# Softmax heads: the probabilities go unscaled through the product with v, whose result stands by query, is scaled there and transposed back

## The chip, the core and the metric

The kernel is one program on one core of a Trainium2 chip. Its time is the device time of one execution in microseconds (us), a median over several runs. The engines are named as the profile names them: PE is TensorE (matmuls and transposes), PEld its weight loads, DVE is VectorE, ACT is ScalarE, POOL is GpSimd, SP is SyncE, which here issues DMAs.

## The reference, cut to what matters

The whole computation is two transformer blocks over 512 positions of width 1024, in float32. The change lies in the softmax heads of the second block: the four heads of group A (merged dilated causal attention), four of group C (a window of 128 with a sink logit), four of group D (causal blocks) and the four heads of the cross attention into 256 memory tokens. Each computes, with heads of 64 columns:

```python
s = jnp.einsum("bgrnqe,bgnke->bgrnqk", qb, kb) * SCALE + bias[None, :, :, None]
s = jnp.where(valid, s, NEG)
m = jnp.maximum(jnp.max(s, axis=-1, keepdims=True), sink)
p = jnp.exp(s - m)
den = jnp.sum(p, axis=-1, keepdims=True) + jnp.exp(sink - m)
o = jnp.einsum("bgrnqk,bgnke->bgrnqe", p / den, vb)
```

(this is group C; A and D have no sink, the cross attention neither sink nor bias). `p / den` may be taken before the product with v or after it, since `den` belongs to a query.

## The kernel before

Everything is float32. A product of float32 precision is made of three matmuls: both factors are split in a high and a low part (`split`, ACT copies the high part, DVE subtracts), and high*high, high*low and low*high are added up in PSUM (`mm3` and the three matmuls of line 1251). Activations are held with features on the 128 partitions and positions along the row.

`softmax_units` makes one head as four units of 128 queries, two to a pair. A unit goes through these steps, parted by `yield`: (1) two matmuls give the scores with the queries on the partitions (`sc`, line 1206), DVE adds the bias and takes the maximum (1211, in the cross attention 1214); (2) ACT takes the exponent and its sum `den` (1218, 1215), DVE takes the reciprocal of `den` (1223) and multiplies the 128 to 512 probabilities of each query by it (1224); (3) PE transposes the probabilities in blocks of 128 keys to a PSUM tile `tr` (1228); (4) they are split into `pth` and `ptl` (105, 106); (5) for the second unit of a pair, the product with v: v (64 columns) is the stationary operand, the probabilities of both units, 256 queries wide where both see the key block and 128 where one does, are the moving one (1252). The result stands with the head's 64 features on the partitions, as the output projection needs it, and ACT copies it to `y` (1254).

A causal head (A, D) has windows of 1, 2, 3 and 4 key blocks; a head of C has 1, 2, 2 and 2; one of the cross attention 2 each. The `tr` tiles have three PSUM buffers, the scores two.

`weave` (line 1314) starts one unit per step, moves the others that are under way by one step each, and between them issues pieces of "fill": the projections of later groups (`pair`, lines 1393 to 1398), the norm of earlier ones (`finish`), or output projections. So the order of the text is that of the weave; a scheduler then moves instructions of each engine within what dependencies allow. The groups come in the order B (another kind of head, unchanged), A, D, C, and then, in `cross`, the memory heads. In the profiled execution the scores of the changed heads start at 952 us; roughly, A stands before 1000, D from 1000 to 1031, C from 1031 to 1072 with its last steps up to 1080, the cross heads from 1102 to 1149. The MLP with its large matmuls follows up to the end.

Line 1363 makes a constant, `lower`, which is read once, at line 1367, long before the heads.

Of the kernel before, what the change touches and what calls it, by code (L numbers as in the profile page):

```python
# [11 lines left out]
FT = mybir.dt.float32  # L12
FR = mybir.dt.float32r
AF = mybir.ActivationFunctionType
OP = mybir.AluOpType
# [4 lines left out]
P = 128  # L20
# [43 lines left out]
class Net:  # L64
# [1117 lines left out]
    def softmax_units(self, q, ks, v, vc, y, yr, window, bias=None, sink=None, keys=SEQ, tag=lambda pair: pair,  # L1182
                      again=False):

        nc = self.nc
        V = nc.vector
        vh, vl = v
        nkt = keys // P  # L1190
        st = {}

        def unit(ti):
            pair, i = divmod(ti, 2)
            wins = [window(2 * pair + n) for n in range(2)]
            k0, k1 = wins[i]
            f0 = wins[0][0]
            w = (k1 - k0) * P
            if bias is not None and (ti == 0 or again and i == 0):
                st["e"] = self.bt.tile([P, 512], FT, name="bias")  # L1200
                nc.sync.dma_start(st["e"], bias)
            ps = self.psc.tile([P, 512], FT, name="sc")
            qs, q0 = q(pair)
            qs = qs[:, q0 + i * P:q0 + i * P + P]
            for x in range(2):
                nc.tensor.matmul(ps[:, 0:w], qs, ks[x][:, k0 * P:k1 * P], start=x == 0, stop=x == 1)
            p = self.at.tile([P, keys], FT, name="e")[:, 0:w]
            nm, den = (self.at.tile([P, 1], FT, name=n) for n in ("nm", "den"))
            if bias is not None:
                o = 384 - P * ti + P * k0  # L1210
                V.tensor_tensor_reduce(p, ps[:, 0:w], st["e"][:, o:o + w], -1.0, 3.0e38 if sink is None else sink[1],
                                       OP.add, OP.min, nm)
            else:
                V.tensor_reduce(nm, ps[:, 0:w], AX.X, OP.max, negate=True)
                nc.scalar.activation(p, ps[:, 0:w], AF.Exp, bias=nm, accum_out=den)
            yield
            if bias is not None:
                nc.scalar.activation(p, p, AF.Exp, scale=-1.0, bias=nm, accum_out=den)
            if sink is not None:
                e = self.at.tile([P, 1], FT, name="es")  # L1220
                nc.scalar.activation(e, sink[0], AF.Exp, bias=nm)
                V.tensor_tensor(den, den, e, OP.add)
            V.reciprocal(den, den)
            V.tensor_scalar(p, p, den, None, OP.mult)
            yield
            pt = self.ptr.tile([P, 512], FT, name="tr")
            for j in range(k1 - k0):
                nc.tensor.transpose(pt[:, j * P:(j + 1) * P], p[:, j * P:(j + 1) * P], self.ident)
            yield
            if i == 0:  # L1230
                n = wins[1][1] - f0
                k = tag(pair)
                full = 1280 if k and keys == SEQ else 512
                st["p"] = [self.ap.tile([P, full], FR, name=f"{t}{k}")[:, 0:256 * n].rearrange(
                    "p (j t) -> p j t", j=n) for t in ("pth", "ptl")]
            pth, ptl = st["p"]
            src = pt[:, 0:w].rearrange("p (j t) -> p j t", t=P)
            at = (slice(None), slice(k0 - f0, k1 - f0), slice(i * P, (i + 1) * P))
            self.split(pth[at], ptl[at], src)
            if i == 0:  # L1240
                return
            yield
            yp = self.ptr.tile([P, 512], FT, name="tr")

            (a0, a1), (b0, b1) = wins
            both = [j for j in range(nkt) if a0 <= j < a1 and b0 <= j < b1]
            jobs = [(j, 0, 256) for j in both]
            jobs += [(j, 0, P) for j in range(a0, a1) if j not in both]
            jobs += [(j, P, 256) for j in range(b0, b1) if j not in both]
            for ji, (j, c0, c1) in enumerate(jobs):  # L1250
                for x, (m, d) in enumerate(((vh, pth), (vh, ptl), (vl, pth))):
                    nc.tensor.matmul(yp[0:64, c0:c1], m[:, j, vc:vc + 64], d[:, j - f0, c0:c1], start=ji == x == 0,
                                     stop=ji == len(jobs) - 1 and x == 2)
            nc.scalar.activation(y[yr, pair * 256:pair * 256 + 256], yp[0:64, 0:256], AF.Copy)

        return [unit(i) for i in range(4)]

    def stick_units(self, q, ks, v, vc, y, yr):
# [83 lines left out]
    def hybrid(self):  # L1342
        nc = self.nc
        V = nc.vector
        I = self.I
        with ExitStack() as es:
# [3 lines left out]
            yp = self.pool(e2, "yp", 1)  # L1350
# [8 lines left out]
            c = hp  # L1359
            self.strict = c.tile([P, P], FT, name="strict")  # L1360
            nc.gpsimd.affine_select(self.strict, self.ones, pattern=[[1, P]], compare_op=OP.is_gt, fill=0.0, base=0,
                                    channel_multiplier=-1)
            lower = c.tile([P, P], FT, name="lower")
            nc.gpsimd.affine_select(lower, self.ones, pattern=[[-1, P]], compare_op=OP.is_ge, fill=0.0, base=0,
                                    channel_multiplier=1)
            self.ntri = c.tile([P, P], FR, name="ntri")
# [605 lines left out]
```

## Time and profile before

| | |
|---|---|
| median of three runs | 1522.76 us (1522.1 to 1524.31) |
| profiled execution, device time | 1525.71 us |
| its span in the trace | 1524.0 us |
| PE busy | 1464.5 us, 96% of the span |
| PEld busy | 1319.5 us, 87% |
| DVE busy | 1007.3 us, 66% |
| ACT busy | 741.2 us, 49% |
| granted TensorE clock over the span | 0.994 |

Busy time of an engine is the time covered by at least one of its records. Matmuls overlap: one of 256 columns shows some 0.28 us, while the next starts 0.12 us later. So a busy PE can still have room, and what a matmul costs is read from the distance between the starts of neighbours, not from its own length. A weight load (PEld) stands ahead of each matmul and overlaps the matmul before.

### The profile page before, as it was taken

How to read it: one execution, taken by the hardware profiler on the slowest of the kernel's cores; microseconds unless marked ns; L12 is line 12 of the kernel's file. 1: busy time of each engine (PE TensorE's matmuls, PEld its weight loads, DVE VectorE, ACT ScalarE, POOL GpSimd, SP SyncE). 2: the span in 40 equal slices, each digit the busy share in tenths (PEclk: the TensorE clock that was granted, in tenths of full speed). 3: DMA queues.
4: the chain of work that ended last, by engine and by line, in shares of the span. 5: the costliest groups of instructions: out<-in, count | busy, mean ns of one | idle time of the engine just before them, and what ended most of it. 6: DMA issues, size and time to landing. Idle time of an engine off the chain costs nothing.

```text
span 1524.0 us, 25154 instructions
## 1 busy us (share of the span) xinstructions
PE 1464.5 (96%) x9769; PEld 1319.5 (87%) x9769; DVE 1007.3 (66%) x1963; ACT 741.2 (49%) x1437; POOL 284.0 (19%) x321
## 2 busy tenths in 40 slices
PE   7899899999989999999999999999989999999996
PEld 7899899988989999989999988988888888888886
DVE  6988979878587766665474755888896443344334
ACT  5333356655665444444454465686685431144321
POOL 1157821003352111100131211000221000000001
PEclk9999999999999999999999999999999999999998
DMA  6333342226546766643657244314211322233221
GB/s 207 100 100 98 103 114 89 65 69 225 162 140 221 255 229 245 226 136 110 184 155 237 99 152 140 124 43 146 97 57 56 97 96 93 88 98 97 97 83 56
DMA packets 76223, 197.63 MB, mean 130 GB/s; under 512 B 16188, under 2 KB 25644, under 8 KB 75976
## 3 DMA queue, kind: packets, MB, share of 16 engines
q1 hardware_dynamic: 67384, 166.66, 34.9%
q0 software_dynamic: 7632, 28.31, 4.9%
q8 instruction: 77, 1.26, 0.3%
q10 hardware_dynamic: 1088, 1.05, 0.2%
q14 instruction: 42, 0.34, 0.1%
HBM read 171.75 MB, written 28.15 MB: 131 GB/s over the span
## 4 chain that ended last, share of the span: by engine, by line
PE 65%; DVE 7%; ACT 3%; DMA 2%; issue 1%; DVEq 0%; SPq 0%; ACTq 0%
PE mm L146 6%; PE mm L147 6%; PE mm L149 6%; PE mm L176 5%; PE mm L179 5%; PE mm L178 5%; PE mx L176 4%; PE mx L179 4%; PE mx L178 4%; PE mx L146 3%; PE mx L147 3%; PE mx L149 3%; PE mm L1396 2%; PE mm L1395 2%; PE mm L1393 2%; DVE xl L109 1%
## 5 line engine op out<-in xcount | busy, mean ns | idle before, releaser
L127 DVE TENSOR_TENSOR wlo<-wst,whi 128x1024 fp32r<-128x1024 f32 (+3 forms) x244 | 299.2, 1228 | 193.1 <-ACT whi L126 116.9
L126 ACT ACTIVATE whi<-wst 128x1024 fp32r<-128x1024 f32 (+3 forms) x244 | 249.9, 1026 | 283.6 <-PE mm L147 113.8
L178 PE MATMUL mm<-xh,whi 128*128 128x256 f32 (+4 forms) x800 | 229.2, 312 | 3.0 <-DVE vl L109 1.6
L179 PE MATMUL mm<-xl,whi 128*128 128x256 f32 (+4 forms) x800 | 229.6, 313 | 0.2
L178 PE MATMUL mx<-xh,whi 128*128 128x512 f32 (+3 forms) x576 | 174.2, 325 | 8.2 <-ACT xh L108 8.2
L179 PE MATMUL mx<-xl,whi 128*128 128x512 f32 (+3 forms) x576 | 175.0, 326 | 1.3 <-DVE xl L109 1.2
L178 PEld LDWEIGHTS mm<-xh,whi 128*128 128x128 f32 (+1 forms) x800 | 150.6, 188 | 13.0 <-DVE vl L109 1.8
L179 PEld LDWEIGHTS mm<-xl,whi 128*128 128x128 f32 (+1 forms) x800 | 150.2, 188 | 10.5 <-issue 0.6
L176 PE MATMUL mm<-xh,wlo 128*128 128x256 f32 (+4 forms) x800 | 138.2, 312 | 0.0
L146 PE MATMUL mm<-hh,whi 128*128 128x256 f32 (+1 forms) x480 | 132.6, 307 | 0.0
L147 PE MATMUL mm<-hl,whi 128*128 128x256 f32 (+1 forms) x480 | 132.5, 307 | 0.0
L178 PEld LDWEIGHTS mx<-xh,whi 128*128 128x128 f32 x576 | 109.2, 190 | 17.1 <-ACT xh L108 8.5
L176 PEld LDWEIGHTS mm<-xh,wlo 128*128 128x128 f32 (+1 forms) x800 | 115.3, 187 | 9.9 <-issue 0.4
L179 PEld LDWEIGHTS mx<-xl,whi 128*128 128x128 f32 x576 | 108.8, 189 | 11.9 <-DVE xl L109 2.8
L176 PE MATMUL mx<-xh,wlo 128*128 128x512 f32 (+3 forms) x576 | 104.3, 322 | 0.0
L146 PEld LDWEIGHTS mm<-hh,whi 128*128 128x128 f32 x480 | 90.4, 189 | 5.4
L147 PEld LDWEIGHTS mm<-hl,whi 128*128 128x128 f32 x480 | 90.5, 189 | 5.1
L176 PEld LDWEIGHTS mx<-xh,wlo 128*128 128x128 f32 x576 | 86.0, 187 | 9.1
L252 POOL TENSOR_TENSOR nacc<-nacc,sq 128x256 f32<-128x256 f32 (+2 forms) x58 | 56.2, 970 | 202.2 <-ACT sq L251 193.0
L149 PE MATMUL mm<-hh,wlo 128*128 128x256 f32 (+1 forms) x480 | 79.5, 307 | 1.3 <-DVE wlo L127 1.3
L149 PEld LDWEIGHTS mm<-hh,wlo 128*128 128x128 f32 x480 | 67.5, 188 | 6.7 <-DVE wlo L127 1.7
L252 POOL TENSOR_TENSOR acc<-acc,sq 128x264 f32<-128x264 f32 (+1 forms) x6 | 4.3, 741 | 335.3 <-ACT sq L251 335.3
(570 smaller groups left out, 3305.7 us busy)
## 6 DMA issues: line engine op xcount, KB each, us to landing
wst<-in_w_in_dram SPq DMA_DIRECT2D x39, 512.0 KB, 3.5
wst<-in_w_down_dram SPq DMA_DIRECT2D x32, 512.0 KB, 3.5
wst<-in_w_mup_dram SPq DMA_DIRECT2D x32, 512.0 KB, 3.5
wst<-in_w_mdown_dram SPq DMA_DIRECT2D x32, 512.0 KB, 3.7
wst<-in_w_gate_dram SPq DMA_DIRECT2D x22, 512.0 KB, 4.0
wst<-in_w_up_dram SPq DMA_DIRECT2D x22, 512.0 KB, 3.5
wst<-in_w_out_dram SPq DMA_DIRECT2D x20, 512.0 KB, 3.9
ready<-phi POOLq DMA_DIRECT2D x17, 512.0 KB, 3.1
```

What stands on the lines that cost most here:

```text
L126: nc.scalar.activation(hi[:, 0:n], st[:, 0:n], AF.Copy)
L127: nc.vector.tensor_tensor(lo[:, 0:n], st[:, 0:n], hi[:, 0:n].bitcast(FT), OP.subtract)
L146: nc.tensor.matmul(ps, ah, bh, start=start and i == 0, stop=False)
L147: nc.tensor.matmul(ps, ah, bl, start=False, stop=False)
L149: nc.tensor.matmul(ps, al, bh, start=False, stop=stop and i == n - 1)
L176: nc.tensor.matmul(ps, wl[:, k], xh, start=False, stop=k == KT - 1)
L178: nc.tensor.matmul(ps, wh[:, k], xh, start=k == 0, stop=False)
L179: nc.tensor.matmul(ps, wh[:, k], xl, start=False, stop=False)
L252: (nc.vector if k % len(accs) else nc.gpsimd).tensor_tensor(acc[:, c:c + w], acc[:, c:c + w], sq, OP.add)
L1393: nc.tensor.matmul(ps, wl[:, k], xh, start=False, stop=k == KT - 1)
L1395: nc.tensor.matmul(ps, wh[:, k], xh, start=k == 0, stop=False)
L1396: nc.tensor.matmul(ps, wh[:, k], xl, start=False, stop=False)
```

## The change

The reciprocal and the multiplication of the probabilities go, and with them one `yield`, so the transposes come in the same step as the exponent. The sums of a pair's two units are kept side by side in one tile `den` of two columns. The product is turned: the probabilities of one unit and one key block, 128 queries, are the stationary operand, v's 64 columns the moving one, so the result has the queries on the partitions, 64 columns for each of the two units. The reciprocal of both sums is taken at once, DVE multiplies the result by it on its way out of PSUM to `yt`, and two transposes bring it back to 64 features by 128 queries each, in the upper half of the same `tr` tile, from where ACT copies it as before. `lower` moves to a buffer of the bias tiles.

```diff
-            nm, den = (self.at.tile([P, 1], FT, name=n) for n in ("nm", "den"))
+            nm = self.at.tile([P, 1], FT, name="nm")
+            if i == 0:
+                st["den"] = self.at.tile([P, 2], FT, name="den")
+            dens = st["den"]
+            den = dens[:, i:i + 1]
...
-            V.reciprocal(den, den)
-            V.tensor_scalar(p, p, den, None, OP.mult)
-            yield
             pt = self.ptr.tile([P, 512], FT, name="tr")
...
             yield
+
             yp = self.ptr.tile([P, 512], FT, name="tr")
-
-            (a0, a1), (b0, b1) = wins
-            both = [j for j in range(nkt) if a0 <= j < a1 and b0 <= j < b1]
-            jobs = [(j, 0, 256) for j in both]
-            jobs += [(j, 0, P) for j in range(a0, a1) if j not in both]
-            jobs += [(j, P, 256) for j in range(b0, b1) if j not in both]
-            for ji, (j, c0, c1) in enumerate(jobs):
-                for x, (m, d) in enumerate(((vh, pth), (vh, ptl), (vl, pth))):
-                    nc.tensor.matmul(yp[0:64, c0:c1], m[:, j, vc:vc + 64], d[:, j - f0, c0:c1], start=ji == x == 0,
-                                     stop=ji == len(jobs) - 1 and x == 2)
-            nc.scalar.activation(y[yr, pair * 256:pair * 256 + 256], yp[0:64, 0:256], AF.Copy)
+            for n, (j0, j1) in enumerate(wins):
+                for j in range(j0, j1):
+                    for x, (m, d) in enumerate(((vh, pth), (vl, pth), (vh, ptl))):
+                        nc.tensor.matmul(yp[:, 64 * n:64 * n + 64], d[:, j - f0, n * P:(n + 1) * P],
+                                         m[:, j, vc:vc + 64], start=j == j0 and x == 0, stop=j == j1 - 1 and x == 2)
+            V.reciprocal(dens, dens)
+            yield
+            yt = self.at.tile([P, 2, 64], FT, name="yt", bufs=2)
+            V.tensor_tensor(yt, yp[:, 0:128].rearrange("p (n c) -> p n c", n=2),
+                            dens.unsqueeze(2).to_broadcast([P, 2, 64]), OP.mult)
+            yield
+            for n in range(2):
+                nc.tensor.transpose(yp[0:64, 256 + n * P:256 + (n + 1) * P], yt[:, n], self.ident)
+            nc.scalar.activation(y[yr, pair * 256:pair * 256 + 256], yp[0:64, 256:512], AF.Copy)
...
-            lower = c.tile([P, P], FT, name="lower")
+            lower = bt.tile([P, 512], FT, name="bias")[:, 0:P]
```

In the built program PE has 232 matmuls and transposes more, DVE 64 instructions fewer; the other engines have as many as before. Lines of the changed kernel are four higher after the change, some within it lower; 1248 are its products, 1250 the reciprocal, 1253 the scaling, 1257 the transposes back.

On PE, the product of the first pair of the first A head, before (`e` are the probabilities, `pth` and `ptl` their split transposes, `v2h` and `v2l` the parts of v, `sc` scores):

```order
L1228 MATMUL tr<-ident,e 128x128 x3
L1252 MATMUL tr<-pth_11310,v2h 64x256
L1206 MATMUL sc<-kh,qs 128x512
L1252 MATMUL tr<-ptl_11311,v2h 64x256
L1252 MATMUL tr<-pth_11310,v2l 64x256
L1252 MATMUL tr<-pth_11310,v2h 64x128
L1252 MATMUL tr<-ptl_11311,v2h 64x128
L1252 MATMUL tr<-pth_11310,v2l 64x128
L1228 MATMUL tr<-ident,e 128x128 x4
```

and the start of the same product now:

```order
L1397 MATMUL mm<-xh_8559,wlo 128x512
L1397 MATMUL mm<-xh_8560,wlo 128x512
L1228 MATMUL tr<-ident,e 128x128 x3
L1248 MATMUL tr<-v2h,pth_11287 128x64
L1248 MATMUL tr<-v2l,pth_11287 128x64
L1248 MATMUL tr<-v2h,ptl_11288 128x64
```

Six matmuls of 256 or 128 columns have become nine of 64 (the three at the end of the piece stand three times in a row), in one block.

On PE in the D heads, around the second pair of one head, now (`yt` is the scaled result, `rs` the norm of an earlier group):

```order
L1228 MATMUL tr_11782<-ident_78,e_11723 128x128 x2
L1228 MATMUL tr_11805<-ident_78,e_11788 128x128 x3
L305 MATMUL rs_12590<-ident_78,rsr_12581 128x128 x4
L1257 MATMUL tr_11754<-ident_78,yt_11800 64x128 x2
L1205 MATMUL sc_12105<-kh_11628,qs_11501 128x256
L1205 MATMUL sc_12105<-kl_11629,qs_11501 128x256
L1205 MATMUL sc_12153<-kh_11628,qs_11501 128x384
L1205 MATMUL sc_12153<-kl_11629,qs_11501 128x384
L1248 MATMUL tr_11839<-v2h_10546,pth0_11777 128x64
```

Between a product and its transposes back stand the transposes of later units; between those and the next product, four score matmuls.

On DVE, in the A heads, before:

```order
L1211 ISA e,nm<-sc,bias 128x384
L1211 ISA nm 128x1
L1223 RECIPROCAL den<-den 128x1
L1224 TENSOR_SCALAR e<-e,den 128x256
L1223 RECIPROCAL den<-den 128x1
L1224 TENSOR_SCALAR e<-e,den 128x384
```

and now, at the first scaling of a result:

```order
L1250 RECIPROCAL den<-den 128x2
L1214 ISA e,nm<-sc,bias 128x384
L1214 ISA nm 128x1
L106 TENSOR_TENSOR ptl_11359<-tr,pth_11358 128x3x128
L1253 TENSOR_TENSOR yt<-tr,den 128x128
L1214 ISA e,nm<-sc,bias 128x512
```

Two operations for each unit have become two for each pair, and they have moved from ahead of the transposes to behind the product.

## Rows read from the trace of the kernel before

**Rows 1.** The page: the span, busy time and share of two engines, and the chain of work that ended last, by engine.
```profile
span 1524.0 us, 25154 instructions
PE 1464.5 (96%) x9769; PEld 1319.5 (87%) x9769; DVE 1007.3 (66%) x1963; ACT 741.2 (49%) x1437; POOL 284.0 (19%) x321
...
PE 65%; DVE 7%; ACT 3%; DMA 2%; issue 1%; DVEq 0%; SPq 0%; ACTq 0%
```

**Rows 2.** The view of busy time by stretch: stretch in us, its length, busy time and instructions of PE, PEld, DVE, ACT and POOL, granted clock, DMA share, GB/s. In turn: the A heads, the D heads, the C heads, the passage to the cross attention, the cross heads, the MLP.
```profile
950.00:1000.00 50.00, 50.00 (x326) 44.68 (x325) 39.46 (x114) 31.45 (x80) 2.39 (x6) 1.00 0.32 108
...
1000.00:1031.00 31.00, 29.22 (x214) 25.29 (x213) 29.56 (x103) 26.46 (x75) 0.00 (x0) 1.00 0.14 42
...
1031.00:1072.00 41.00, 39.21 (x254) 33.29 (x252) 34.45 (x119) 28.67 (x90) 0.00 (x0) 1.00 0.43 135
...
1072.00:1102.00 30.00, 27.05 (x217) 25.17 (x218) 25.49 (x62) 19.47 (x50) 8.16 (x10) 1.00 0.34 114
...
1102.00:1146.00 44.00, 40.18 (x312) 36.70 (x311) 40.75 (x119) 34.30 (x103) 10.29 (x13) 1.00 0.17 56
...
1160.00:1500.00 340.00, 340.00 (x1496) 276.05 (x1495) 136.02 (x166) 109.99 (x146) 4.28 (x6) 1.00 0.28 89
```

**Rows 3.** The timeline in the A heads: start in us, length, engine, line, operation, operands (active rows * weight columns, then the moving operand). Two projection matmuls of 512 columns, products with v of 256 and of 128, and five transposes.
```profile
994.22 0.40 PE L1395 MATMUL mm<-xh,whi 128*128 128x512 f32 x1
...
994.45 0.40 PE L1396 MATMUL mm<-xl,whi 128*128 128x512 f32 x1
...
996.43 0.27 PE L1252 MATMUL tr<-pth,v2h 128*64 128x256 f32 x1
...
996.54 0.28 PE L1252 MATMUL tr<-ptl,v2h 128*64 128x256 f32 x1
...
997.13 0.22 PE L1252 MATMUL tr<-pth,v2h 128*64 128x128 f32 x1
...
997.19 0.22 PE L1252 MATMUL tr<-ptl,v2h 128*64 128x128 f32 x1
...
997.31 0.73 PE L1228 MATMUL tr<-ident,e 128*128 128x128 f32 x5
```

**Rows 4.** The timeline elsewhere, of narrow matmuls: eight with 128 weight columns and 66 moving ones in the first block (their matmuls, and their weight loads), and two weight loads of 128 columns followed by one of 64 and the next in the B heads.
```profile
104.42 1.00 PE L528 MATMUL tr<-uc,q 128*128 128x66 f32 x8
...
104.32 0.97 PEld L528 LDWEIGHTS tr<-uc,q 128*128 128x128 f32 x8
...
906.88 0.19 PEld L1289 LDWEIGHTS tr<-ptl,nones 128*128 128x128 f32 x1
906.99 0.14 PEld L1307 LDWEIGHTS tr<-pth,v2h 128*64 128x64 f32 x1
907.05 0.19 PEld L1275 LDWEIGHTS sc<-qs,kh 128*128 128x128 f32 x1
```

**Rows 5.** The view of line 1252, the products with v: length of one in ns (least, median, most), first and last start, shapes with their counts. `v2h` and `v2l` are A, D and C, `xv` the cross heads (both parts of v in one tile).
```profile
L1252 PE MATMUL tr<-pth,v2h x68: 220/277/362, 975.1 to 1079.4; 128*64 128x256 f32 x40, 128*64 128x128 f32 x28
...
L1252 PE MATMUL tr<-ptl,v2h x68: 219/277/334, 975.5 to 1079.5; 128*64 128x256 f32 x40, 128*64 128x128 f32 x28
...
L1252 PE MATMUL tr<-pth,v2l x68: 222/276/284, 975.6 to 1079.5; 128*64 128x256 f32 x40, 128*64 128x128 f32 x28
...
L1252 PE MATMUL tr<-pth,xv x32: 274/280/362, 1114.7 to 1148.4; 128*64 128x256 f32 x32
...
L1252 PE MATMUL tr<-ptl,xv x16: 276/280/334, 1117.4 to 1148.3; 128*64 128x256 f32 x16
```

**Rows 6.** Groups of DVE instructions from 950 to 1146 us, shapes kept apart: count, busy us, mean ns of one, idle time before.
```profile
L1224 DVE TENSOR_SCALAR e<-e,den 128x256 f32<-128x256 f32 x36 | 14.0, 394 | 0.4
...
L1223 DVE RECIPROCAL den<-den 128x1 f32<-128x1 f32 x64 | 9.5, 156 | 4.0 <-ACT e L1218 3.5
...
L1224 DVE TENSOR_SCALAR e<-e,den 128x512 f32<-128x512 f32 x8 | 3.8, 480 | 0.1
...
L1224 DVE TENSOR_SCALAR e<-e,den 128x128 f32<-128x128 f32 x12 | 3.4, 282 | 0.1
L106 DVE TENSOR_TENSOR ptl<-tr,pth 128x128 fp32r<-128x128 f32 x12 | 3.4, 280 | 0.0
...
L1224 DVE TENSOR_SCALAR e<-e,den 128x384 f32<-128x384 f32 x8 | 3.3, 418 | 0.1
```

**Rows 7.** Groups of PE instructions, shapes kept apart, of two stretches: of the D heads (1000 to 1031 us) the first and the last of 23 rows, of the cross heads (1102 to 1146 us) the three rows of its fifteen whose moving operand isn't 256 columns wide.
```profile
L1228 PE MATMUL tr<-ident,e 128*128 128x128 f32 x40 | 6.8, 279 | 0.2 <-ACT y L1254 0.2
...
L1395 PE MATMUL mm<-xh,whi 128*128 128x512 f32 x1 | 0.4, 389 | 0.0
...
L1228 PE MATMUL tr<-ident,e 128*128 128x128 f32 x32 | 5.9, 276 | 0.5 <-ACT o L1254 0.2 <-DVE e L1224 0.2
...
L290 PE MATMUL rs<-ones,nacc 128*128 128x1 f32 x8 | 1.0, 229 | 0.0
L305 PE MATMUL rs<-ident,rc 128*128 128x128 f32 x4 | 0.6, 275 | 0.0
```

**Rows 8.** The view of waits: who waited for whom, us in total, times, longest; PE from 1000 to 1160 us and DVE from 1000 to 1146.
```profile
PE sc L1206 <- DVE nm L1211: 1.5, 5, 0.5
...
DVE e L1211 <- PE tr L1228: 4.9, 3, 2.7
```

More of the change, by code (lines that the diff above doesn't have):

```diff
@@ L1189, in softmax_units @@
         vh, vl = v
-        nkt = keys // P
         st = {}
```

## The prediction

> **What bounds the kernel now.** I read four views, from coarse to fine. The page first: PE is busy in 96% of the span and stands in 65% of the chain that ended last, DVE in 7% [rows 1]. Then busy time by stretch, because the change lies in an eighth of the span alone (950 to 1149 us, by the first and last products and the stretches) [rows 2]. The reader is to see three things there. In the A heads (950 to 1000 us) PE is busy for 50.00 of 50 us and DVE for 39.46: these heads are woven into projections, and PE has nothing to spare. In the D, C and cross heads both are nearly full: PE 29.22, 39.21 and 40.18 against DVE 29.56, 34.45 and 40.75, of 31, 41 and 44 us. And from 1160 us on PE is full for 340 of 340 us, so a delay of the heads isn't made up later: what the heads' stretches gain or lose is the whole effect. The granted clock is 1.00 in all of them, so durations need no correction. Third, the timeline for the price of a matmul, as the distance between starts [rows 3]. Last, the waits: PE's own are small and spread (1.5 us for its largest kind, scores that wait for DVE's maxima, in five pieces), so there is no one long stall that a shorter chain would set free [rows 8].
>
> **The prices on PE.** From start to start a matmul of 512 columns takes 0.23 us (994.22 to 994.45), one of 256 takes 0.117 (I take the middle of 0.11 and 0.12, as 996.43 to 996.54 is rounded), one of 128 with 64 weight columns 0.06 (997.13 to 997.19). Five transposes take 0.73 us, of which the last one's length is some 0.27, so 0.11 each [rows 3].
>
> What the change adds, 64 moving columns against 128 weight columns, doesn't occur before. The nearest rows: eight matmuls of 66 columns with 128 weight columns take 1.00 us, and their eight loads 0.97 us; without the last one's 0.19 that is 0.78 over seven, 0.11 each. In the B heads a load of 128 columns is followed by the next load 0.11 us later (906.88 to 906.99), one of 64 columns 0.06 later (906.99 to 907.05) [rows 4]. So a load costs by its columns, and the narrow matmul can't run faster than its load: 0.11. From below, if only the moving columns counted, it would cost no more than the 0.06 of today's narrowest product. I take 0.11: it rests on two places, one with the same kind of operand (`pth`/`ptl` type) on the loading side. The turned product makes v, the narrow factor, the moving one, and the wide factor the one that is loaded.
>
> A rule of the Trainium skill says otherwise: "TensorE: Matmul & The Clock Gate", section "Weight-path perf modes", states that weights are loaded several at a time when there are 128 of them and the type is not FP32 (about twice as fast in its measurement). If the rounded float32 type of `pth` counted as not FP32, the change would turn slow loads of 64 columns into fast loads of 128; the load at 906.88, of 128 columns, with the next 0.11 us later, speaks against it, and the case is the third rival below.
>
> **The sum on PE.** Before [rows 5]: 3 x 40 + 32 + 16 = 168 products of 256 columns and 3 x 28 = 84 of 128. 168 x 0.117 + 84 x 0.06 = 19.7 + 5.0 = 24.7 us. After: three matmuls for each unit and key block. A causal head has 1 + 2 + 3 + 4 = 10 blocks, so 30; eight of them 240. A head of C has 7 blocks, 21; four of them 84. A cross head 8 blocks, 24; four of them 96. In all 420 x 0.11 = 46.6 us (with 0.111). Two transposes for each of 32 pairs: 64 x 0.109 = 7.0 us. So PE gets 46.6 + 7.0 - 24.7 = 28.9 us more work. By group: A and D 8.0 each (per head 3.33 + 0.44 - 12 x 0.117 - 6 x 0.06 = 2.0), C 6.1, cross 6.8.
>
> **The sum on DVE.** Gone are 64 reciprocals, 9.5 us, and 64 multiplications, 14.0 + 3.8 + 3.4 + 3.3 = 24.5 us. Added are 32 reciprocals of two columns (0.156, as of one column) and 32 scalings of 128 x 128 out of PSUM; the nearest rows are 0.280 (a subtraction of that size from PSUM) and 0.282 (the old multiplication of that size) [rows 6]. That is 32 x 0.436 = 14.0 us. DVE gets 34.0 - 14.0 = 20.0 us free, 5.3 of it in each causal group of four heads. ACT has the same copies as before.
>
> **What of it is hidden.** A: PE is full, so the 8.0 us are on the path. Cover for the rest is what PE has free, and the busy time hides part of it, so I count slots. Cross heads: of 312 instructions [rows 2] 32 transposes and 4 of line 305 at 0.109, 8 of line 290 at 0.111 (a load of 128 columns), the other 268 of 256 columns at 0.117 [rows 7]: 3.9 + 0.9 + 31.4 = 36.2 of 44 us, 7.8 free, twice the 3.8 that the stretch shows idle. D heads by the same view: of 214, 60 transposes at 0.109, 32 bound by a 128-column load at 0.111, 56 of 256, 24 of 128 with 64 weight columns, 8 of 384 at 0.175, 34 of 512 at 0.232, together 27.4 of 31, 3.6 free [rows 2, 7]. For C I take the idle 1.8 twice over, 3.6 (an estimate from the other two). The passage to the cross heads (2.95 idle) holds norms and projections and lends nothing.
>
> If all of this room is filled, the added work costs 8.0 in A, 8.0 - 3.6 = 4.4 in D, 6.1 - 3.6 = 2.5 in C and nothing in the cross heads: 15 us. If none is filled, 28.9. DVE's relief is what makes filling possible: in D it falls from 29.6 to about 24.3 of 31 us, so the waits for maxima [rows 8] should shrink. What is late next is PE itself, and a new handoff in each pair: product, DVE scaling, transposes back, ACT copy. Behind waiting transposes back stand PE's scores and the next product, and the next product needs the `tr` buffer that this copy frees (three buffers; a pair's result is now held for three steps of the weave, before for one). The chain that goes (reciprocal 0.16, multiplication 0.28 to 0.48) is about as long as the one that comes (0.16, 0.28, two transposes); other units cover most of it. For the 24 pairs outside A I put 0.2 us each, the smallest waits of the view (1.5 us in five, and single ones of 0.2 in the groups [rows 7]), 24 x 0.2 = 5 us. In A, fill covers it.
>
> `lower` in a bias buffer: it is read long before the first bias tile is loaded; nothing. If that read came late, the first bias load on SP would wait, and the weight loads queued behind it.
>
> So 15 + 5 = 20 us. The profiled execution's span of 1524.0 becomes 1544, its time of 1525.71 becomes 1546 (1.7 around the span). It stood 2.95 above the median, so the median goes from 1522.76 to 1543.
>
> **Rivals.**
> - *The room is filled completely.* DVE no longer holds D and the cross heads back and the new handoffs hide behind other units: +15, down to +8 if C's tail, where PE's idle time runs on to 1080 us, takes in the rest of C's and some of D's work. For it: DVE is at 29.56 of 31 and 40.75 of 44. Against: the idle bits are small and come from many causes [rows 7, 8]. Time 1531 to 1538.
> - *Nothing is filled and the handoffs add waits.* PE queues its work in order, and a result tile is held three times as long in three buffers: 28.9 + 32 x 0.2 = 35, so 1558 at most; 1549 to 1558. For it: DVE's longest wait now is already for transposes (4.9 us in three [rows 8]). Against: the order puts transposes of other units and scores between each product and its transposes back.
> - *The weight loads of 128 columns turn out cheap.* Then a product costs 0.06: 420 x 0.06 = 25.2, and with 7.0 for the transposes back PE gets only 25.2 + 7.0 - 24.7 = 7.5 us more, of which A keeps 1.9; the rest is less than the 15.0 us free in D, C and cross, and with DVE's 20.0 us gone these could end up to 9.4 earlier. Between 1.9 - 9.4 = -7.5 and +7.5: 1515 to 1530, in the middle no change. It decides from a product's price of (24.7 - 7.0 + 15.0)/420 = 0.078 us downwards. Against it stand both places of [rows 4].
> - *The change doesn't do what it says*: that the scheduler leaves the old order. The built order shows 64 reciprocals and 64 multiplications gone, and the new blocks in place, so I give it nothing.
>
> **How the numbers follow.** My forecast (+14 to +26) 0.60; room filled completely 0.18; nothing filled 0.13; cheap loads 0.08, half of it faster by more than 0.2% (3 us, about what a measurement of this kernel tells from no change), a quarter within; 0.01 for anything else. The forecast's own range is 1537 to 1549. Down to 1531 it takes in most of the first rival, up to 1554 half of the second: about 0.8 together. Faster 0.05, same 0.04, slower 0.91.
>
> **What would show it.** In the profile after: loads of the products (line 1248) 0.11 us apart within a block of 9 or 21; PE with 10001 matmuls, and slots of 2.3 us for a block of 21; DVE some 20 us less busy; the A heads about 8 us longer, D and C each about 5, the cross heads 2 to 3. Wrong it would be if products stand 0.06 apart, if the A heads don't lengthen, or if PE's waits for line 1257 or for the `tr` buffer come to more than 10 us.

## The result, and the profile after

The changed kernel takes 1546.62 us (four runs, 1543.96 to 1548.83) against 1523.53 us of the kernel before on the same chips, a ratio of 1.0148 with an interval of 1.0134 to 1.0161: 23 us slower, where 20 were forecast (1543, range 1531 to 1554). The profiled execution took 1548.83 us, its span was 1547.1.

The page of the changed kernel, the lines of [rows 1]:

```profile
span 1547.1 us, 25597 instructions
...
PE 1493.8 (97%) x10001; PEld 1353.6 (87%) x10001; DVE 996.4 (64%) x1899; ACT 744.7 (48%) x1437; POOL 284.8 (18%) x321
...
PE 67%; DVE 6%; DMA 2%; ACT 1%; issue 1%; SPq 0%; DVEq 0%; ACTq 0%
```

PE has its 232 instructions more and gained in the chain (65 to 67%); DVE is 11 us less busy over the whole span, of which the two added groups say how much they cost:

```profile
L1253 DVE TENSOR_TENSOR yt<-tr,den 128x128 f32<-128x128 f32 x32 | 9.2, 288 | 15.6 <-PE tr L1248 15.2
...
L1250 DVE RECIPROCAL den<-den 128x2 f32<-128x2 f32 x32 | 5.2, 161 | 3.0 <-ACT e L1221 1.5 <-ACT e L1218 1.3
```

Together 14.4 us, priced at 14.0. With the 34.0 us of the groups that are gone DVE should be 19.6 us less busy, and the page has 10.9. The same 56 instructions at line 109 take 2.0 us more than before (37.9 against 35.9); the rest lies in many small groups and in how instructions overlap, and wasn't attributed. The column behind the second bar shows a new wait: DVE idles 15.2 us before the scalings until products are done. The other way round, PE's waits from 950 to 1175 us have none for a maximum any more, which was PE's largest kind before [rows 8].

The price of a product, as weight loads in a block of 21 (start, length; compare [rows 4]):

```profile
1019.83 0.19 PEld L1248 LDWEIGHTS tr<-v2l,pth 128*128 128x128 f32 x1
1019.94 0.19 PEld L1248 LDWEIGHTS tr<-v2h,ptl 128*128 128x128 f32 x1
1020.05 0.19 PEld L1248 LDWEIGHTS tr<-v2h,pth 128*128 128x128 f32 x1
1020.17 0.19 PEld L1248 LDWEIGHTS tr<-v2l,pth 128*128 128x128 f32 x1
```

They start 0.11 us apart. Two of the three loads of a triple take the same `pth` (the third and fourth rows here, one behind the other; the first row is such a second load too); the second is no cheaper for it, as from the first row to the next it is 0.11 us again.

Busy time by stretch, with the columns of [rows 2]: A, then D's time, then the end of C in four pieces, then the cross heads.

```profile
950.00:1000.00 50.00, 50.00 (x334) 45.23 (x332) 32.41 (x88) 30.36 (x76) 2.87 (x6) 1.00 0.31 106
1000.00:1031.00 31.00, 30.97 (x235) 28.88 (x235) 22.45 (x73) 21.26 (x59) 0.00 (x0) 1.00 0.15 43
...
1077.00:1080.50 3.50, 3.50 (x18) 3.03 (x17) 2.60 (x15) 2.54 (x10) 0.00 (x0) 0.51 0.46 147
1080.50:1094.10 13.60, 12.00 (x88) 9.62 (x87) 9.36 (x30) 9.24 (x28) 0.00 (x0) 1.00 0.01 2
1094.10:1101.00 6.90, 6.90 (x34) 6.66 (x33) 2.94 (x9) 2.77 (x8) 0.00 (x0) 0.51 0.00 0
...
1125.00:1169.00 44.00, 42.30 (x366) 41.87 (x366) 37.35 (x96) 33.65 (x100) 11.23 (x13) 1.00 0.16 51
```

Two things are to be seen. From 1000 to 1031 us PE went from 29.22 to 30.97 busy and DVE from 29.56 to 22.45: PE's idle time there is gone and PE alone is the bound, as forecast. And in two pieces the granted clock is 0.51, the lower of TensorE's two levels (half clock below), for 3.4 and 6.8 us; before, no stretch of the heads showed that.

Where the 23 us arose is read from first and last starts. Before: first score of A 952.1, first of C 1028.1, first of the cross heads 1102.1, last copy of theirs 1148.7. After, the tile of scores (count: least/median/longest ns, first and last start):

```profile
L1205 PE MATMUL sc<-kh,qs x48: 221/341/582, 953.2 to 1084.2; 128*128 128x256 f32 x20, 128*128 128x128 f32 x12, 128*128 128x384 f32 x8, 128*128 128x512 f32 x8
...
L1205 PE MATMUL sc<-xk,qs x32: 278/282/365, 1125.3 to 1158.2; 128*128 128x256 f32 x32
```

line 1258's cross copies of the changed kernel:

```profile
L1258 ACT ACTIVATE o<-tr x8: 361/376/379, 1139.6 to 1168.7; 64x256 f32<-64x256 f32 x8
```

and, from its timeline, C's first score:

```profile
1040.00 0.30 PE L1205 MATMUL sc<-kh,qs 128*128 128x128 f32 x1
```

| stretch | before | after | difference |
|---|---|---|---|
| A and D, first score to C's first | 76.0 | 86.8 | +10.8 |
| C and passage, to the first cross score | 74.0 | 85.3 | +11.3 |
| cross heads, to the last copy | 46.6 | 43.4 | -3.2 |
| from there to the end | 375.3 | 378.4 | +3.1 |

That makes 22.0, and 1.1 lie ahead of the heads. The borders are starts of instructions, and work moves across them. Behind C's first score run 144 of the new products, of which C has 84, so half of D's 120 run there; before, it was 107, with 60 of C's. The columns are as in [rows 2], PE and PEld alone, of the products' line, first before, then after:

```profile
1028.05:1102.10 74.05, 13.60 (x107) 10.98 (x107) 1.00 0.38 122
...
953.20:1040.00 86.80, 21.38 (x180) 21.54 (x180) 1.00 0.23 74
1040.00:1125.30 85.30, 18.20 (x144) 18.02 (x144) 0.94 0.34 109
```

And in the cross heads, where the change adds 64 instructions to PE, the stretch has only 27 more, so other work of PE went behind them: their -3.2 and the +3.1 after them belong together.

```profile
1102.10:1148.70 46.60, 42.78 (x334) 39.30 (x333) 41.20 (x120) 34.63 (x104) 10.29 (x13) 1.00 0.16 52
...
1125.30:1168.70 43.40, 41.70 (x361) 41.27 (x360) 37.08 (x96) 33.08 (x99) 11.23 (x13) 1.00 0.16 50
```

### The profile page after: what moved, and what is told of

It reads as the page before. It is cut to its first block, busy times and chain, and to the rows that moved or that the text cites. A ratio compares the mean times of both kernels' runs of the same rounds, so it can differ in the third digit from the quotient of the medians.

```text
span 1547.1 us, 25597 instructions
## 1 busy us (share of the span) xinstructions
PE 1493.8 (97%) x10001; PEld 1353.6 (87%) x10001; DVE 996.4 (64%) x1899; ACT 744.7 (48%) x1437; POOL 284.8 (18%) x321
## 4 chain that ended last, share of the span: by engine, by line
PE 67%; DVE 6%; DMA 2%; ACT 1%; issue 1%; SPq 0%; DVEq 0%; ACTq 0%
PE mm L146 6%; PE mm L147 6%; PE mm L149 6%; PE mm L178 5%; PE mm L176 5%; PE mm L179 5%; PE mx L176 4%; PE mx L179 4%; PE mx L178 4%; PE tr L1248 3%; PE mx L146 3%; PE mx L147 2%; PE mx L149 2%; PE mm L1397 2%; PE mm L1400 2%; PE mm L1399 2%
```

## The experiments

Three theories stood against each other. L: a product costs its weight load, PE's work decides. W: the new handoffs (product, scaling, transposes back, copy, with three `tr` buffers) make the delay. K, formed when the half clock was seen: the 64 narrow columns let the clock fall. In single expectations D stands for DVE holding the D and cross heads back, N for chance. All ratios are to the kernel before, run beside it.

**The width of the moving operand** (e5, repeated as e5_again), and the changed kernel a second time (e10).

```diff
-nc.tensor.matmul(yp[:, 64 * n:64 * n + 64], d[...], m[:, j, vc:vc + 64], ...)
+nc.tensor.matmul(yp[:, P * n:P * n + P], d[...], m[:, j, vc // P * P:vc // P * P + P], ...)
```

(DVE then scales the half that belongs to the head.)

> The changed kernel with 128 moving columns in place of 64 in each product (v of two heads; the other head's half isn't used), so the 420 loads stay and the matmuls get twice as wide. Theory L: the load of 0.111 us hides a matmul of 0.06, no change: 1544 to 1549. If the moving columns count: 420 x 0.03 = 12 us slower, about 1558.

> The changed kernel, unaltered, a second time, beside the kernel before on one chip. Its profile showed TensorE at half clock for 3.4 us from 1077 us and for 6.8 us from 1094 us, inside the C heads' end, while the variant with 128 moving columns (e5) showed none there. Theory K (64 moving columns keep the array so little occupied that the clock falls): it shows half clock among the heads again, and is 5 to 6 us slower than e5: ratio to before 1.014 to 1.016. Theory N (chance): none there this time, and the ratio comes down to that of e5, 1.010 to 1.013.

> The variant with 128 moving columns, unaltered, a second time, as the base of the three beside it. Theory K (the clock): again no half clock among the heads, and a ratio to before of 1.010 to 1.013, clear of the changed kernel's 1.0148 and 1.0167. Theory N (its gain was chance): 1.014 or more, or half clock there.

Measured: e5 1541.47 us, ratio 1.0114 (1.0098 to 1.0129); e5_again 1543.54, 1.0111 (1.0096 to 1.0126); e10 1549.92, 1.0167 (1.0147 to 1.0186). Twice the columns cost nothing, which is L's reading: the load hides them. That they gained 5 to 8 us none had expected. e10 shows the half clock at the same places as the first profile, e5 none among the heads, e5_again 6.8 us of it (first e10, then e5_again, in stretches):

```profile
1077.10:1080.50 3.40, 3.40 (x16) 2.96 (x16) 2.68 (x14) 2.66 (x11) 0.00 (x0) 0.50 0.48 155
1094.20:1101.00 6.80, 6.80 (x32) 6.56 (x32) 3.06 (x9) 2.47 (x8) 0.00 (x0) 0.50 0.00 0
```

```profile
1088.60:1095.40 6.80, 6.80 (x31) 6.56 (x32) 2.95 (x11) 2.60 (x7) 0.00 (x0) 0.50 0.00 0
```

e5 and e5_again are the same program, so they price it. From C's first score to the first cross score e5 takes 1117.0 - 1037.1 = 79.9 us, e5_again 1120.2 - 1037.2 = 83.0. C's first score of e5 in its timeline, then its cross scores in the view of the tile:

```profile
1037.08 0.31 PE L1205 MATMUL sc<-kh,qs 128*128 128x128 f32 x1
```

```profile
L1205 PE MATMUL sc<-xk,qs x32: 278/282/365, 1117.0 to 1150.0; 128*128 128x256 f32 x32
```

6.8 us at half clock go with 3.1 us more, measured on one pair of executions. By that the changed kernel's 10.2 cost some 5 (an estimate; its own 85.3 us of the table against e5's 79.9 is 5.4). Why the clock falls isn't shown. K expected none in e5_again, and there was one; and in e7 below, whose A, D and C are in the old form, two pieces of 3.4 us lie among those heads (stretches of e7):

```profile
1017.90:1021.30 3.40, 3.40 (x16) 2.91 (x15) 1.87 (x9) 1.02 (x6) 0.00 (x0) 0.50 0.18 67
1065.70:1069.10 3.40, 3.40 (x18) 3.28 (x19) 3.04 (x17) 2.59 (x12) 0.00 (x0) 0.50 0.51 166
```

The scheduler also ordered some of C's instructions otherwise in e5, so e5's whole gain isn't put down to the clock.

**One of three terms left out** (e4 of the changed kernel, e4 wide of e5).

```diff
-for x, (m, d) in enumerate(((vh, pth), (vl, pth), (vh, ptl))):
+for x, (m, d) in enumerate(((vh, pth), (vh, ptl))):
```

> The changed kernel with two of the three matmuls of each product with v (the low part of v is left out): 140 matmuls fewer, the same steps, waits and buffers. Theory L: 140 x 0.111 = 15.5 us less work on PE, of which about four fifths (23.1/28.9) count: 12 us faster than the changed kernel, about 1535. Theory W (the new handoffs product, scaling, transposes back, copy make the delay): 0 to 4 us faster, 1543 to 1547.

> e5 with two of the three matmuls of each product (the low part of v left out), so that the clock is out of the comparison: 15.5 us less work on PE, nothing else. Theory L: three fifths of it count, as 17 of 28.9 us do in e5: 9 us faster than e5, ratio to before about 1.005. Theory W (handoffs): 0 to 3 us faster than e5, 1.009 or more.

Measured: e4 1539.62 us, 1.0097 (1.0078 to 1.0116); e4 wide 1533.63, 1.0055 (1.0035 to 1.0075). Against the changed kernel's 1.0148 e4 gains 0.0051, 8 us of the 12 expected; its profile has half clock for 13.6 us among the heads, 3.4 more than the changed kernel's. Against e5_again's 1.0111 the wide one gains 0.0056, 8.5 us where L said 9 and W 0 to 3. The clock wasn't out of this comparison, as its expectation hoped, but it is the same on both sides: e4 wide, too, has 6.8 us of half clock among the heads.

```profile
1066.10:1072.90 6.80, 6.80 (x33) 6.18 (x33) 4.56 (x26) 4.02 (x17) 0.00 (x0) 0.50 0.37 119
```

All handoffs were kept, so W falls as the main cause: PE's work it is.

**The transposes back left out** (e2, and e2 wide).

```diff
-for n in range(2):
-    nc.tensor.transpose(yp[0:64, 256 + n * P:256 + (n + 1) * P], yt[:, n], self.ident)
-nc.scalar.activation(y[yr, pair * 256:pair * 256 + 256], yp[0:64, 256:512], AF.Copy)
+for n in range(2):
+    nc.scalar.activation(y[yr, pair * 256 + n * P:pair * 256 + (n + 1) * P], yt[0:64].rearrange("p n c -> p (n c)"), AF.Copy)
```

> The changed kernel without the two transposes back of each pair: ACT copies the scaled result as it lies (queries where features should be, half of the queries left out), in two copies instead of one. Theory L: 64 x 0.109 = 7.0 us less on PE, some 5 to 7 of it counting: 1540 to 1542. Theory W: a hop of the handoff in each of 32 pairs goes too, so 10 us or more: 1537 or less.

> e5 without the two transposes back of each pair (the result is copied as it lies, in two copies; half of the queries left out): Theory L: 7.0 us less on PE, about 4 us faster than e5, 1.008 to 1.009. Theory W: a hop goes in each of 32 pairs, 8 us or more: 1.006 or less.

Measured: e2 1541.91 us, 1.0120 (1.0102 to 1.0138), e2 wide 1542.98, 1.0105 (1.0089 to 1.0122). The first is 4 us below the changed kernel, the second 1 us below e5_again with intervals that overlap. As measured, both stay short of W's 10 and 8 us. But the half clock among the heads differs here: 20.4 us in e2's profile against 10.2 in the changed kernel's, and 10.2 in e2 wide's against 6.8 in e5_again's (below, e2, then e2 wide). At 3.1 us for 6.8, an estimate, e2 gains some 9 and e2 wide 2.6: the first is nearer to W, the second to L. So this pair doesn't decide between them, nor whether the 7.0 us of transposes count by three fifths, all the more as the edit gives ACT 32 copies more; what speaks against W is e4 wide.

```profile
1023.20:1030.00 6.80, 6.80 (x29) 6.22 (x28) 2.73 (x12) 2.24 (x8) 0.00 (x0) 0.50 0.16 42
1081.20:1084.60 3.40, 3.40 (x17) 3.22 (x16) 2.00 (x9) 2.36 (x8) 0.00 (x0) 0.51 0.00 0
1088.10:1094.90 6.80, 6.80 (x32) 6.62 (x31) 3.21 (x10) 2.64 (x9) 0.00 (x0) 0.50 0.01 2
1142.70:1146.10 3.40, 3.15 (x15) 3.15 (x15) 3.21 (x9) 2.34 (x8) 0.00 (x0) 0.50 0.00 0
```

```profile
1023.10:1029.90 6.80, 6.80 (x27) 6.22 (x26) 3.66 (x16) 2.82 (x12) 0.00 (x0) 0.50 0.10 26
1087.90:1091.30 3.40, 3.40 (x17) 3.11 (x16) 1.77 (x6) 3.40 (x9) 0.00 (x0) 0.50 0.00 0
```

**The old form kept in A, or everywhere but in the cross heads** (a flag picks the old lines; both on e5).

```diff
+64 * h, y, yr, causal, e, turned=name != "A")
...
+turned = keys != SEQ
```

> The variant with 128 moving columns (e5), but the A heads in the old form (probabilities scaled, v stationary), so 96 x 0.111 + 1.7 us of transposes less 7.0 us of old products. The prediction's stage sum (A full on PE, 8.0 us on the path): 8 us faster than e5, ratio to before about 1.005 to 1.008. If A hides its share as the others do: 3 us or less faster, 1.009 or more.

> The turned product, 128 moving columns wide, in the cross heads alone; A, D and C as before. The prediction's stage sum (7.8 us free there for 6.8 of added work, DVE relieved by 4.6): within 3 us of before, ratio 0.998 to 1.002. If added PE work counts in every stage: 5 to 7 us slower, 1.003 to 1.005.

Measured: e6 1536.72 us, 1.0082 (1.0065 to 1.0098), 4.5 to 5 us below e5, between the two expectations. Its trace puts A's share higher, at 6.8 us: from 952.2 to C's first score it takes 80.0 us, e5 from 950.3 86.8. C's first score of e6 in its timeline, and the scores of A and C in the view of the tile:

```profile
1032.17 0.30 PE L1205 MATMUL sc<-kh,qs 128*128 128x128 f32 x1
```

```profile
L1205 PE MATMUL sc<-kh,qs x48: 219/338/504, 952.2 to 1073.4; 128*128 128x256 f32 x20, 128*128 128x128 f32 x12, 128*128 128x384 f32 x8, 128*128 128x512 f32 x8
```

That the median shows less may be the clock: e6's trace stood at half clock for 10.2 us ahead of the heads and e5's for 3.4, and its A starts 1.9 us later. What is left over the 76.0 of before, 4.0 us, is D's up to C's first score. (The 96 loads in the expectation are a slip: four heads of 30 make 120, and with these the sum gives its 8 us.) e7 took 1527.56 us, 1.0008 (0.9995 to 1.0022): in the cross heads alone the turned form costs nothing that can be measured, as the sum over the stages had it.

**What DVE's relief is worth**: nothing scaled at all, in the old form (e1, the lines below), and the old scaling kept beside the turned product (e3 wide, which puts these lines and their step back into e5).

```diff
-            V.reciprocal(den, den)
-            V.tensor_scalar(p, p, den, None, OP.mult)
```

> The kernel before without the reciprocals and the multiplications of the probabilities, so the heads' results stay unnormalised (that part is left out): DVE has 34 us less to do (64 x 0.156 + 24.5), PE the same. Theory L (PE's work decides, each narrow product costs its weight load): DVE's relief alone is worth little, since A is full on PE: 3 to 8 us faster than before, 1515 to 1521. Theory D (DVE holds the D and cross heads back): 10 us faster or more, 1513 or less.

> e5 with the old scaling of the probabilities on DVE kept (reciprocal, multiplication and a step of the weave in each unit; the result is copied to yt without another scaling), so DVE has 29 us more than in e5. If DVE's relief is what lets PE's room be filled: 8 us or more slower than e5, ratio 1.016 or more. If it is worth as little as in e1: 0 to 4 us slower, 1.011 to 1.014.

Measured: e1 1521.09 us, 0.9976 (0.9966 to 0.9986), 3.7 us faster: L. That is what the scaling costs in the old form. e3 wide 1548.74, 1.0149 (1.0120 to 1.0179), 6 us slower than e5_again, between the two expectations and with the widest interval of all. Part of the 6 us may be the clock: the two slower of its four executions had mean granted clocks of 0.989 and 0.990, the others 0.993 and 0.995. The stages of the profiled execution, one of the faster two, are cleaner, as neither it nor e5 had half clock among the heads (e3 wide, then e5, with the borders of the table):

```profile
950.70:1037.60 86.90, 86.69 (x612) 78.92 (x612) 70.66 (x222) 55.27 (x147) 2.27 (x5) 1.00 0.23 74
1037.60:1119.50 81.90, 76.46 (x552) 68.84 (x551) 63.40 (x195) 51.77 (x144) 8.14 (x10) 1.00 0.36 113
1119.50:1166.50 47.00, 45.16 (x373) 43.05 (x372) 42.97 (x125) 33.61 (x101) 10.08 (x13) 1.00 0.15 46
```

```profile
950.30:1037.08 86.78, 86.67 (x612) 78.89 (x612) 58.83 (x175) 55.30 (x147) 2.27 (x5) 1.00 0.24 74
1037.08:1117.00 79.92, 75.97 (x552) 68.72 (x551) 58.81 (x170) 51.50 (x144) 8.13 (x10) 1.00 0.36 116
1117.00:1162.10 45.10, 43.44 (x372) 42.43 (x370) 37.24 (x101) 33.93 (x101) 10.92 (x13) 1.00 0.16 48
```

Up to C's first score DVE has 12 us more to do and the time is the same; C and the passage take 2.0 us more, the cross heads 1.9. So some 4 us stand against 29 us of DVE's work, where the old form had 3.7 against 34: that the relief pays more in the turned form isn't shown.

**Another way to scale**: the transposes multiply by a diagonal (e8).

```diff
-V.tensor_scalar(p, p, den, None, OP.mult)
+diag = self.at.tile([P, P], FT, name="diag", bufs=2)
+nc.gpsimd.tensor_scalar(diag, self.ident, den, None, OP.mult)
...
-nc.tensor.transpose(pt[...], p[...], self.ident)
+nc.tensor.matmul(pt[...], p[...], diag, start=j == 0, stop=j == k1 - k0 - 1)
```

> The kernel before with the scaling put into the transposes: POOL builds a diagonal of the reciprocals (128 x 128), and the probabilities are multiplied by it on PE in place of the identity, at the same 0.11 us each; DVE loses the 64 multiplications (24.5 us), PE's work stays, POOL gets 64 operations. By e1 (3.7 us for all of DVE's 34) no more than 3 us faster: 0.998 to 1.000. If POOL's longer operation stands in each unit's chain: up to 5 us slower, 1.003.

Measured: 1530.15 us, 1.0041 (1.0026 to 1.0057). POOL's operation takes 0.60 us, twice the one of that size on DVE (0.28 [rows 6]), and stands in the chain of every unit; that this makes the 6 us wasn't shown, as PE and its loads idle for `diag` only 1.1 us in all.

```profile
L1225 POOL TENSOR_SCALAR diag<-ident,den x64: 594/603/1641, 958.5 to 1145.8; 128x128 f32<-128x128 f32 x64
```

No version that computes the whole reference beat the kernel before.

## Why the prediction was right

*The price of a product*: right. 0.11 us by the loads, and no wider for twice the columns (e5). So the 46.6 us of products and the 28.9 us of added work stand, and the rival of cheap loads is out.

*A full on PE, 8.0 us on the path*: 6.8 by e6's trace. *Cross heads, nothing*: e7 says so.

*D, 4.4, and C, 2.5*: mis-sized, too little together. As half of D's products run behind C's first score, the two can't be parted there. D takes 4.0 us up to it (e6); from it to the first cross score e5, without half clock, takes 79.9 us against 74.0 before, 5.9 more, and e6 80.0. That is 9.9 us where 6.9 were forecast: of the 14.1 us of added work 4.2 were hidden, not the 7.2 of room that was counted (3.6 in D) and estimated (3.6 in C). Which of the two was too large isn't shown.

*The handoffs, 24 x 0.2 = 5 us*: too much, as far as the view of waits tells. PE's waits in the changed kernel from 950 to 1175 us show 0.6 us for line 1257 and 0.5 for the products; a delay shorter than a matmul's own length needn't show there as idle time, so some of the 3 us that D and C took above their forecast may be of this kind.

```profile
PE tr L1257 <- DVE yt L1253: 0.6, 1, 0.6
PE tr L1248 <- DVE ptl L106: 0.5, 1, 0.5
```

*The granted clock needs no correction*: right for the rows of before, wrong for the changed kernel, and worth some 5 us. So the sum of 20 came near 23 partly by luck: 5 us of handoffs, of which 1.1 were seen, stand in for 5 us of half clock that weren't foreseen. Worked out from the stages, 6.8 + 9.9 + 0 + 5 is 21.7, and the table has 22.0.

*DVE's relief makes filling possible*: not seen in D up to C's first score, and D it was said for. With the old scaling kept (e3 wide) DVE is busy 70.7 in place of 58.8 us up to C's first score, and the time is 86.9 against 86.8. What the relief gives, some 4 us, lies in C, the passage and the cross heads.

Two of the signs that were named didn't come: DVE is 10.9 us less busy, not 20, and the cross heads didn't get 2 to 3 us longer.

## What to carry to other kernels

When a matmul is turned round, count its weight loads: the narrow factor belongs on the stationary side, and a wide one that must be loaded for a few columns costs its load, here 0.11 us for 64 and for 128 moving columns alike. Work taken from an engine that is busy beside a full one (34 us of DVE for 3.7 us of time) wasn't worth 28.9 us of work on the full one. Free slots are not yet hidden work: of 7.2 us counted and estimated in D and C 4.2 were used. And before times of one execution each are compared by stages, see which work moved across the borders and where the clock fell.

## What the runs showed of the hardware that was not expected

TensorE's granted clock fell to its lower level for 3.4 or 6.8 us at a time while PE was busy: in the changed kernel the second time after 13.6 us with PE busy for 12.0 of them, and twice at the same places in two profiles taken apart; 6.8 us of it went with 3.1 us more. In the old form the heads had idled more at full clock, so how much PE idled in such a stretch doesn't by itself tell when the clock falls; what does, no run here separated.

```profile
1060.00:1080.00 20.00, 16.50 (x130) 13.67 (x130) 18.06 (x69) 15.97 (x56) 0.00 (x0) 1.00 0.19 64
```

Nor is half clock a matter of the changed kernel alone: the profiled execution of every kernel here has some. The kernel before has three pieces of 3.4 us ahead of its heads (from 60.8, 316.8 and 839 us; the last is shown) and the last 9.2 us of its span, in which PE has no instruction any more.

```profile
839.00:842.40 3.40, 3.24 (x15) 3.24 (x16) 1.55 (x2) 0.00 (x0) 0.00 (x0) 0.50 0.99 363
...
1514.80:1524.00 9.20, 0.00 (x0) 0.00 (x0) 4.82 (x11) 0.35 (x1) 1.82 (x2) 0.50 0.62 219
```

The changed kernel has 10.2 us ahead of the heads too, so between these two profiles the 10.2 among the heads are the difference. From one execution of a program to the next the pieces can change: e5 has one of 3.4 us ahead of the heads, e5_again two of 3.4 there and the 6.8 among the heads. So a difference of some 3 us between single executions of two of these kernels can be clock alone.
